# A two-block transformer kernel: modulation sums in the projection stage, an eighth early expert load, key products among transposes, and products moved from VectorE to ScalarE

## The chip, the cores and the metric

The kernel runs on one core of a Trainium2 chip. The metric is the time of one execution on the device in microseconds (us), the median of several runs. One execution is also taken by the hardware profiler, and all rows below come from that one. The engines are TensorE (PE; its weight loads are PEld), VectorE (DVE), ScalarE (ACT), GpSimd (POOL) and SyncE (SP, which here only issues DMAs). Data live in SBUF and in the matmul banks (PSUM).

## What is computed

Two blocks in a row on 512 latent tokens of width 1024, with 256 context tokens, in fp32. Cut to what the change touches:

```python
def first_block(x, c, ctx, c_ctx, w_mod, b_mod, ...):
    m_lat = split(silu(c) @ w_mod + b_mod, 6)        # six vectors of 1024 for the latent
    m_ctx = split(silu(c_ctx) @ w_mod + b_mod, 6)    # six for the context
    h_lat = modulate(rmsnorm(x), m_lat[0], m_lat[1]); h_ctx = ...
    mix   = token_mixers(h_lat @ w_in, h_ctx @ w_in) # neighbourhood and differential attention, gated deltanet, Fourier mix
    x = x + m_lat[2] * (mix @ w_out)
    h = modulate(rmsnorm(x), m_lat[3], m_lat[4])
    x = x + m_lat[5] * expert_choice_ffn(h, w_router, w_gate, w_up, w_down)   # 16 experts, 64 tokens each
    return rmsnorm(x)

def second_block(x, c, ctx, c_ctx, w_mod_2, ...):
    sh1, sc1, gt1, sh2, sc2, gt2 = split(silu(c) @ w_mod + b_mod, 6)          # shifts and scales of the context: only the first two
    h = rmsnorm(x) * (1 + sc1) + sh1;  p = h @ w_in
    y_ssd = ssd_bidir(p)         # chunked scan in both directions: scores = (C B^T) * exp(decay)
    y_att = softmax(q k^T, window, context keys, sink) v
    x = x + gt1 * merge(y_ssd, y_att)
    x = x + gt2 * conv_ffn(rmsnorm(x) * (1 + sc2) + sh2)
    return rmsnorm(x)
```

Vectors 3 and 4 of both modulations are wanted for the latent alone.

## The kernel before, in words

The program runs through stages, each a Python generator that writes instructions; `weave` (L321) takes the generators of a stage in turn, always the one with the smallest sum of the fractions that it has yielded so far. That order, and a scheduler that sorts by readiness within it, decide what stands behind what on each engine; every engine then runs its own queue strictly in order. The stages that matter, with their times in the profiled execution:

- **Projection**, about 120 to 221 us, the end of `g_proj` (L701). The input goes through `w_in` in blocks of 256 columns. Each block's weights (the DRAM tensor is `in_cola`, 512 KB a load into `base`) are split into a high and a low fp32r half on ScalarE (cast, L1963) and on VectorE or GpSimd (difference, L1964), and each product is three matmuls, hi·hi, hi·lo, lo·hi. SP issues the raw loads in program order.
- **Fourier mix and neighbourhood attention**, about 221 to 452 us, while the gated deltanet (`g_dn`, 40 rounds of short matmuls on `bank_dn`, a chain from round to round) and the modulation vectors (`g_mods`, L652) run beside it. `g_mods` makes ten vectors of 1024, each in two halves of 512 columns. `mod_rows` (L510) loads a half in four pieces of 512 KB into a ring named `mods` and multiplies the two conditioning columns with it, 8 fp32 matmuls of 32x512 (two records each in the trace) in four row groups; `mod_cols` (L521) turns the four groups with four transposes a half (L528) and adds them up on VectorE; `mod_cols_pk` (L533) does that with eight 64x128 matmuls by the identity into `bigbank`; `mod_bcast` (L545) spreads a vector over the partitions. Each step yields 0.1.
- **Differential attention**, 452 to 640 us, with 56 more rounds of the deltanet, then `w_out` and the router.
- **Experts** (`g_b`, L1617), 741 to 1692 us. Each of the 16 takes twelve loads of 2 MB (`in_w_gate`, `in_w_up`, `in_w_down`). A list `more` hands buffers of finished stages to the ring of loads; seven loads are issued before the first expert starts. `pair` (L1596) gathers the 2 x 64 tokens of two experts with an indirect DMA into a tile `Y` and turns them with 8 transposes. Up to 1297 us the context part of the second block's scan (`g_c0`) runs beside.
- **Tail of the experts** (`c_tile`, L2035), to 1740 us: each of the four token tiles is added to the residual, normed twice, and after the fourth `to_hT2` (L1974) turns all tiles, 32 transposes of 128x128, with scale and shift on ScalarE (L1987), a cast on VectorE (L1989) and a difference on VectorE or GpSimd (L1990). Then `c_att` begins with the keys: `tok2` (L2004), 48 matmuls of 128x256 for two token tiles.
- **Attention and scan of the second block** (`weave(self.c_att(Q), self.c_ssd(Q))`, L2719), 1740 to 2370 us. In `c_att` the softmax weights of two heads are divided by their sums on VectorE (L2171, 64 instructions of 128x512 or 128x640) ahead of their transposes (L2181). In `c_ssd` `weights(k)` (L2418) makes the decay weights of a channel pair and chunk, and `mixed(k)` (L2434) uses them:

```python
nc.scalar.activation(E[:, h], rw[:, h, 1], AF.Identity, bias=gc(1, 1, h))                        # L2424
nc.vector.scalar_tensor_tensor(E[:, h], rw[:, h, 0], gc(1, 0, h), E[:, h], ...)                  # L2426
nc.scalar.activation(E, E, AF.Exp)                                                              # L2427
nc.vector.tensor_scalar(W[:, h], cb[:, c, 0], gc(0, 0, h), None, op0=OP.mult)                    # L2429
nc.vector.scalar_tensor_tensor(W[:, h], cb[:, c, 1], gc(0, 1, h), W[:, h], op0=OP.mult, op1=OP.add)  # L2430
nc.gpsimd.tensor_mul(W, W, E)                                                                   # L2431
```

  `mixed` puts into `bank_y`, for each pair, chunk and head, `xs` times `W` and the chunk's state part `of` times the identity, two fp32 matmuls of 64x128 (two records each in the trace).
- **Output and FFN**, 2370 us to the end.

## Time and profile before

| | |
|---|---|
| median of 3 runs | 2982.91 us (2982.39 to 2989.98) |
| profiled execution: its time | 2982.76 us |
| profiled execution: its span | 2980.9 us |
| PE busy | 2770.4 us, 93% of the span |
| DVE, ACT, POOL busy | 1334.9 us (45%), 902.3 us (30%), 625.7 us (21%) |
| DMA | 658.53 MB, mean 221 GB/s |

Shares over the whole span mix stages with different limits, so the stages are read one by one. In the rows below, "busy" of a group is the time in which at least one of its instructions ran; matmuls are pipelined, so the mean of one is longer than what one adds. The bracket or the text behind the second bar says how long the engine was idle just before these instructions, and what released it. `L399` is the line of the helper that records nearly every matmul, so matmuls are told apart by their tiles.

### The profile page before, as it was taken

How to read it: one execution, taken by the hardware profiler on the slowest of the kernel's cores; microseconds unless marked ns; L12 is line 12 of the kernel's file. 1: busy time of each engine (PE TensorE's matmuls, PEld its weight loads, DVE VectorE, ACT ScalarE, POOL GpSimd, SP SyncE). 2: the span in 40 equal slices, each digit the busy share in tenths (PEclk: the TensorE clock that was granted, in tenths of full speed). 3: DMA queues.
4: the chain of work that ended last, by engine and by line, in shares of the span. 5: the costliest groups of instructions: out<-in, count | busy, mean ns of one | idle time of the engine just before them, and what ended most of it. 6: DMA issues, size and time to landing. Idle time of an engine off the chain costs nothing.

```text
span 2980.9 us, 41808 instructions
## 1 busy us (share of the span) xinstructions
PE 2770.4 (93%) x16824; PEld 1776.0 (60%) x16824; DVE 1334.9 (45%) x2654; ACT 902.3 (30%) x1836; POOL 625.7 (21%) x660
## 2 busy tenths in 40 slices
PE   7999989997999999988888789999999899999998
PEld 4894547765334333332222267777777688888886
DVE  5522445655121211111101167878787854454445
ACT  5511225532111010100000044545454543343333
POOL 3121224531000000000000024232323322332222
PEclk9999999998999999999999999999999999999999
DMA  6216661038999999989999923324242464242331
GB/s 268 75 34 200 209 218 32 30 121 309 397 430 430 429 429 430 429 371 430 431 431 430 387 88 105 118 64 123 72 120 74 134 232 160 94 154 95 97 99 57
DMA packets 213122, 658.53 MB, mean 221 GB/s; under 512 B 13816, under 2 KB 131192, under 8 KB 188352
## 3 DMA queue, kind: packets, MB, share of 16 engines
q1 hardware_dynamic: 185504, 601.73, 52.4%
q10 hardware_dynamic: 26272, 49.93, 4.7%
q0 software_dynamic: 1152, 4.19, 0.3%
q8 instruction: 133, 2.18, 0.3%
q14 instruction: 61, 0.50, 0.1%
HBM read 632.07 MB, written 23.73 MB: 220 GB/s over the span
## 4 chain that ended last, share of the span: by engine, by line
PE 68%; DMA 16%; DVE 10%; issue 2%; ACT 2%; POOL 2%; SPq 1%; ACTq 0%; POOLq 0%; DVEq 0%
PE bank_mm L399 29%; PE bigbank L399 20%; DMA l<-in_w_up 6%; PE bank_pj L399 6%; DMA l<-in_w_down 4%; PE bank_c L399 4%; PE bank_dn L399 2%; DMA mods<-in_cola 2%; DMA l<-in_w_gate 1%; PE bank_sm L399 1%; DVE base L2426 1%; DVE mix L2430 1%; PE bank_dnr L399 1%; DVE mix L2429 1%; PE bank_mm L2181 1%
## 5 line engine op out<-in xcount | busy, mean ns | idle before, releaser
L399 PE MATMUL bank_pj<-c,c 128*128 128x512 f32 (+2 forms) x1368 | 319.7, 376 | 0.3 <-DVE c L1964 0.3
L399 PE MATMUL bank_mm<-c,c 128*128 128x512 f32 (+1 forms) x1608 | 304.4, 347 | 4.9 <-ACT b L1987 3.2
L399 PEld LDWEIGHTS bank_mm<-c,c 128*128 128x128 f32 x1608 | 259.3, 191 | 44.2 <-ACT b L1987 3.6
L399 PE MATMUL bigbank<-l 128*64 128x512 f32 (+1 forms) x1104 | 266.1, 594 | 17.9 <-DMA l<-in_w_up 13.1
L399 PEld LDWEIGHTS bank_pj<-c,c 128*128 128x128 f32 (+1 forms) x1368 | 225.7, 189 | 50.7 <-issue 17.5
L1963 ACT CAST c<-base 128x1024 fp32r<-128x1024 f32 x147 | 152.8, 1045 | 254.3 <-PE bigbank L399 105.7
L1964 POOL TENSOR_TENSOR c<-base,c 128x1024 fp32r<-128x1024 f32 x47 | 116.7, 2483 | 472.9 <-ACT c L1963 404.6
L1964 DVE TENSOR_TENSOR c<-base,c 128x1024 fp32r<-128x1024 f32 x100 | 136.3, 1365 | 136.8 <-ACT c L1963 133.7
L399 PEld LDWEIGHTS bigbank<-l 128*64 128x64 f32 (+1 forms) x1104 | 80.9, 141 | 175.8 <-issue 140.4
L1692 DVE TENSOR_TENSOR b<-l,bigbank 128x512 f32<-128x512 f32 x32 | 20.5, 683 | 340.8 <-PE bigbank L399 293.5
L1691 ACT ACTIVATE l<-bigbank 128x512 f32<-128x512 f32 x32 | 17.4, 595 | 423.7 <-PE bigbank L399 423.7
L399 PE MATMUL bank_mm<-l 128*64 128x512 f32 (+2 forms) x528 | 124.8, 601 | 9.1 <-DMA l<-in_w_down 8.0
L399 PE MATMUL bigbank<-out,c 128*128 128x512 f32 x480 | 113.8, 397 | 1.9 <-ACT out L2524 1.8
L399 PE MATMUL bank_c<-b 128*128 128x256 f32 (+3 forms) x496 | 110.0, 373 | 1.9 <-ACT b L425 0.8
L399 PE MATMUL bank_mm<-h,sp 128*128 128x512 f32 (+3 forms) x544 | 105.5, 382 | 4.3 <-ACT h L644 3.8
L399 PEld LDWEIGHTS bank_dn<-dn 64*64 64x64 f32 x1920 | 74.8, 134 | 55.0 <-issue 39.3
L399 PEld LDWEIGHTS bigbank<-out,c 128*128 128x128 f32 x480 | 91.7, 192 | 23.0 <-ACT out L2524 2.2
L399 PE MATMUL bigbank<-b,l 128*64 128x512 f32 x352 | 84.9, 614 | 21.8 <-DMA b<-in_w_up 10.9
L1717 DVE TENSOR_TENSOR b<-bank_mm,ab 64x512 f32<-64x512 f32 x16 | 10.9, 683 | 208.1 <-PE bank_mm L399 208.1
L1786 ACT ACTIVATE b<-bank_c,base 128x256 f32<-128x256 f32 x20 | 11.3, 563 | 304.6 <-PE bank_c L399 304.6
L399 PEld LDWEIGHTS bank_c<-b 128*128 128x128 f32 (+1 forms) x496 | 80.4, 188 | 37.2 <-issue 23.9
L399 PE MATMUL bigbank<-c,ffn 128*128 128x512 f32 x432 | 100.3, 390 | 0.0
(538 smaller groups left out, 5060.7 us busy)
## 6 DMA issues: line engine op xcount, KB each, us to landing
l<-in_w_up SPq DMA_DIRECT2D x36, 2048.0 KB, 14.6
l<-in_w_down SPq DMA_DIRECT2D x31, 2048.0 KB, 17.0
l<-in_w_gate SPq DMA_DIRECT2D x29, 2048.0 KB, 18.2
mods<-in_cola SPq DMA_DIRECT2D x80, 512.0 KB, 4.9
base<-in_w_in SPq DMA_DIRECT2D x68, 512.0 KB, 3.7
b<-in_w_gate SPq DMA_DIRECT2D x15, 2048.0 KB, 34.0
base<-in_w_gate SPq DMA_DIRECT2D x13, 2048.0 KB, 16.9
wo<-in_w_up SPq DMA_DIRECT2D x13, 2048.0 KB, 33.8
```

The source lines that it names most:

```text
L399: self.mm_ins = self.nc.tensor.matmul(out, l, r, start=start, stop=stop).ins
L1691: nc.scalar.activation(s, ac[0][:, j], AF.Silu)
L1692: nc.vector.tensor_mul(hid[:, 512 * j:512 * j + 512], s, ac[1][:, j])
L1717: nc.vector.tensor_mul(Y[pp, 0:512], dn[0:64], gt2[0:64, 0:512])
L1786: nc.scalar.activation(y, b, AF.Identity, scale=wc(1), bias=self.col(bname, i))
L1963: nc.scalar.copy(hi, raw)
L1964: (nc.vector if self.wn % 4 in self.losplit else nc.gpsimd).tensor_sub(lo, raw, hi.bitcast(F32))
L2181: nc.tensor.transpose(tb[:, z], p[:, 128 * (g0 + z):128 * (g0 + z) + 128], self.ident)
L2426: nc.vector.scalar_tensor_tensor(E[:, h], rw[:, h, 0], gc(1, 0, h), E[:, h], op0=OP.subtract, op1=OP.min)
L2429: nc.vector.tensor_scalar(W[:, h], cb[:, c, 0], gc(0, 0, h), None, op0=OP.mult)
L2430: nc.vector.scalar_tensor_tensor(W[:, h], cb[:, c, 1], gc(0, 1, h), W[:, h], op0=OP.mult, op1=OP.add)
```

## The change

1. **Modulation sums.** Vectors 3 and 4 of both modulations leave `g_mods`. A new generator `g_late_mods` makes their eight halves in `g_proj`, which calls `next(sums)` at 16 places of the projection stage. A half loads eight pieces of 128x512 (256 KB each, on SP, a ring of four buffers); VectorE multiplies and accumulates five of them, ScalarE multiplies three, GpSimd adds these and the two partial sums (`mod_sums`); `mod_close` then sums over the partitions with 8 matmuls of 64x1 or 4 of 128x1 by a column of ones. Only the latent's conditioning column is used. A half is closed one half later. `g_mods` keeps six vectors, in the order 2, 5, then 0, 1, 2, 5 of the second modulation, with a yield of 1/6.
2. **Early load.** `more` gets `out_b` as an eighth buffer; the gather of a pair goes into `gt1_b`, one buffer, and the transposes read it there, so a pair's gather waits for the transposes of the pair before.
3. **Keys.** `c_tile` turns tiles 0 and 1 after the third tile; after the fourth it writes the transposes of tiles 2 and 3 between the 48 key matmuls of tiles 0 and 1 (in a bank `c0`), and ScalarE copies that bank to `self.rr`, which `c_att` then reads.
4. **ScalarE.** The first product of the decay weights (L2429, 128 instructions) and one of the two softmax divisions of each pair of heads (32 of 64) go from VectorE to ScalarE as copies with a scale.
5. **State part.** `mixed` puts `of` into `bank_y` with four 128x128 transposes for each pair, 64 in all, in place of 128 matmuls of 64x128 by the identity; `xs` times `W` accumulates on them.

```diff
-    def mod_cols_pk(self, s, wdram, bi, j, ring, rows, out):
-        nc = self.nc
-        t = self.big().rearrange("p (k g r) -> p k g r", k=8, g=4)
-        for h in range(2):
-            r = rows()
-            self.mod_rows(s, wdram, 2 * j + h, ring, r)
-            for kt in range(8):
-                self.mm(t[64 * h:64 * h + 64, kt].rearrange("p g r -> p (g r)"), r[:, kt::8], self.ident)
-        nc.vector.tensor_reduce(out, t[:, :, :, 0:2].rearrange("p c g r -> p c r g"), AX.X, OP.add)
-        nc.vector.tensor_add(out, out, self.col("b_mod_pk", 8 * bi, 8)[:, :, None].to_broadcast([128, 8, 2]))
...
+    def mod_sums(self, s, wdram, j, rings):
+        nc, (wr, da, pa, pp) = self.nc, rings
+        wv = self.block(wdram, j)
+        d, o = da(), pa()
+        for kt in range(8):
+            w, c = wr(), s[:, kt, 0:1]
+            self.ld(w, wv[:, kt])
+            if kt == 0:
+                nc.vector.tensor_scalar(d, w, c, None, op0=OP.mult)
+            elif kt in (1, 3, 6):
+                z = o if kt == 1 else pp()
+                nc.scalar.activation(z, w, AF.Copy, scale=c)
+                if kt > 1:
+                    nc.gpsimd.tensor_add(o, o, z)
+            else:
+                nc.vector.scalar_tensor_tensor(d, w, c, d, op0=OP.mult, op1=OP.add)
+            if kt == 3:
+                yield
+        nc.gpsimd.tensor_add(o, o, d)
+        self.msum = o
+    def mod_close(self, o, h, bias, out, pk):
+        p, n = (slice(64 * h, 64 * h + 64), slice(0, 8)) if pk else (slice(0, 128), slice(4 * h, 4 * h + 4))
+        t = self.bank((128, 8), "md")
+        for c in range(8 if pk else 4):
+            self.mm(t[p, n.start + c:n.start + c + 1], o[:, c::8] if pk else o[:, c * 128:(c + 1) * 128], self.km("one", 1))
+        self.nc.vector.tensor_add(out[p, n], t[p, n], bias[p, n])
+    def g_late_mods(self, P):
+        s1, s2 = self.s1b.ap(), self.s2b.ap()
+        mp, mc = self.mpk_b.ap(), self.m2c_b.ap()
+        of = [Ring(P, [512], 2, more=[Buf(self.M, [512]) for _ in range(2)])] + [Ring(self.M, [512], n) for n in (1, 2, 1)]
+        owed = []
+        for s, w, j, name, n, out, pk in ((s1, "w_mod", 3, "b_mod_pk", 0, mp[:, 0, :, 0], True), (s1, "w_mod", 4, "b_mod_pk", 8, mp[:, 1, :, 0], True),
+                                          (s2, "w_mod_2", 3, "b_mod_2", 24, mc[:, 2, :, 0], False), (s2, "w_mod_2", 4, "b_mod_2", 32, mc[:, 3, :, 0], False)):
+            for h in range(2):
+                yield from self.mod_sums(s, w, 2 * j + h, of)
+                if owed:
+                    owed.pop()()
+                owed.append(lambda o=self.msum, h=h, n=n, name=name, out=out, pk=pk: self.mod_close(o, h, self.col(name, n, 8), out, pk))
+                yield
+        owed.pop()()
+        for z in of:
+            for b in z.b:
+                b.free()
...
-            self.mod_bcast(s1, wm, I["b_mod"], 2, wr, rows, self.gt1_b.ap(), self.sel)
-            yield 0.1
-            self.mod_cols_pk(s1, wm, 0, 3, wr, rows, mp[:, 0])
-            yield 0.1
-            self.mod_cols_pk(s1, wm, 1, 4, wr, rows, mp[:, 1])
             nc.vector.scalar_tensor_tensor(a2, mp[:, 1, :, 0], 1.0, self.col("norm2_g_pk", 0, 8), op0=OP.add, op1=OP.mult)
-            yield 0.1
-            self.mod_bcast(s1, wm, I["b_mod"], 5, wr, rows, self.gt2_b.ap(), self.sel)
-            yield 0.1
+            for j, g in ((2, self.gt1_b), (5, self.gt2_b)):
+                self.mod_bcast(s1, wm, I["b_mod"], j, wr, rows, g.ap(), self.sel)
+                yield 1 / 6
...
-            for i, j in enumerate((0, 1, 3, 4)):
-                self.mod_cols(s2, wm, "b_mod_2", j, wr, rows, mc[:, i])
-                yield 0.1
+            for j in range(2):
+                self.mod_cols(s2, wm, "b_mod_2", j, wr, rows, mc[:, j])
+                yield 1 / 6
...
+                cr.free()
+                cr2.free()
+                sums = self.g_late_mods(P)
+            if t % 2 == 0:
+                next(sums)
...
-        cr.free()
-        cr2.free()
+        for _ in sums:
+            pass
...
-        nc.gpsimd.indirect_dma_start(Y, None, self.xnd, bass.IndirectOffsetOnAxis(self.ix[:, pr:pr + 1], 0))
+        nc.gpsimd.indirect_dma_start(G, None, self.xnd, bass.IndirectOffsetOnAxis(self.ix[:, pr:pr + 1], 0))
         yield
         for k4 in range(2):
             b = self.bank((128, 4, 128))
             for kk in range(4):
-                nc.tensor.transpose(b[:, kk], Y[:, 4 * k4 + kk::8], self.ident)
+                nc.tensor.transpose(b[:, kk], G[:, 4 * k4 + kk::8], self.ident)
...
-        more = [None, None, sum_b.ap(), None, None, None, in_b.ap()]
+        more = [None, None, sum_b.ap(), None, None, None, in_b.ap(), out_b.ap()]
...
+        mc, a = self.m2c_b.ap(), self.ab2_b.ap()
+        turned = lambda i: self.g_hT2([c["xn"][:, 2 * i], c["xn"][:, 2 * i + 1]], i, a[:, 0], mc[:, 0, :, 0], c["u"], lambda: self.bank((128, 2, 256)))
+        if t == 2:
+            for _ in turned(0):
+                pass
         if t == 3:
-            mc, a = self.m2c_b.ap(), self.ab2_b.ap()
+            last, kb = turned(1), self.bank((128, 2, 256), "c0")
             for i in range(2):
-                self.to_hT2([c["xn"][:, 2 * i], c["xn"][:, 2 * i + 1]], i, a[:, 0], mc[:, 0, :, 0], c["u"], lambda: self.bank((128, 2, 256)))
+                self.tok2(self.pre[0], i, 1, b=kb[:, i:i + 1])
+                for _ in range(3 if i == 0 else 1):
+                    next(last)
+            for _ in last:
+                pass
+            self.cp(self.rr.rearrange("p (t n) -> p t n", t=2), kb, "a")
...
-                b = self.tok2(w, t, 2)
+                b = self.rr.rearrange("p (t n) -> p t n", t=2) if half + t == 0 else self.tok2(w, t, 2)
...
-                for i in range(2):
-                    nc.vector.tensor_scalar(u["p"][i], u["p"][i], ri[:, i:i + 1], None, op0=OP.mult)
+                nc.vector.tensor_scalar(u["p"][0], u["p"][0], ri[:, 0:1], None, op0=OP.mult)
+                nc.scalar.activation(u["p"][1], u["p"][1], AF.Copy, scale=ri[:, 1:2])
...
-                    nc.vector.tensor_scalar(W[:, h], cb[:, c, 0], gc(0, 0, h), None, op0=OP.mult)
+                    nc.scalar.activation(W[:, h], cb[:, c, 0], AF.Copy, scale=gc(0, 0, h))
...
-                    ys[pr] = self.bank((128, 512), "y")
+                    b = ys[pr] = self.bank((128, 512), "y")
+                    for z in range(4):
+                        nc.tensor.matmul(b[:, 128 * z:128 * z + 128], of[:, z, 128 * pr:128 * pr + 128], self.ident, start=z == 0, stop=False, is_transpose=True)
                 yb, W, tk = ys[pr], Ws.pop(k), slice(128 * c, 128 * c + 128)
-                for z in range(2):
-                    for h in range(2):
-                        o = 128 * pr + 64 * h
-                        self.mm(yb[64 * h:64 * h + 64, tk], (of if z else xs)[:, c, o:o + 64], self.ident if z else W[:, h], z == 0, z == 1)
+                for h in range(2):
+                    o = 128 * pr + 64 * h
+                    self.mm(yb[64 * h:64 * h + 64, tk], xs[:, c, o:o + 64], W[:, h], False, c == 3)
```

TensorE in the projection, near its middle; `h_...` and `sp_...` are the split halves of the input and of a weight block, `bank_md` is the bank of the sums. Before:

```order
L399 MATMUL bank_mm<-h_117,sp_350 128x512
L399 MATMUL bank_mm<-h_116,sp_354 128x512
L399 MATMUL bank_mm<-l_105,a_109 128x24 x4
L399 MATMUL bank_mm<-h_118,sp_349 128x256
L399 MATMUL bank_mm<-h_119,sp_349 128x256
```

and now, with one of the eight closes among the matmuls of a block:

```order
L399 MATMUL bank_mm<-h_117,sp_350 128x512
L399 MATMUL bank_mm<-h_116,sp_354 128x512
L399 MATMUL bank_mm<-l_105,a_109 128x24 x4
L399 MATMUL bank_md<-base_59,l_105 64x1 x8
L399 MATMUL bank_mm<-h_118,sp_349 128x256
L399 MATMUL bank_mm<-h_119,sp_349 128x256
```

The other rows kept their places. TensorE at the end of the experts; `b_...` holds the token tiles, `c_...` the split weights of the keys and the split transposed tiles. Before:

```order
L1983 MATMUL bank_mm_9728<-base2_59,b1_6410 128x128
L1983 MATMUL bank_mm_9739<-base2_59,b1_6410 128x128
L1983 MATMUL bank_mm_9728<-base2_59,b1_6410 128x128 x3
L1983 MATMUL bank_mm_9739<-base2_59,b1_6410 128x128 x3
L1983 MATMUL bank_mm_9750<-base2_59,b1_6410 128x128 x4
L1983 MATMUL bank_mm_9761<-base2_59,b1_6410 128x128 x4
L399 MATMUL bank_mm_9830<-c4_9616,c1_9613 128x256
L399 MATMUL bank_mm_9830<-c8_9620,c1_9613 128x256
L399 MATMUL bank_mm_9830<-c4_9616,c2_9614 128x256
```

and now, in a piece of the keys, where the transposes of tiles 0 and 1 are already behind:

```order
L399 MATMUL bank_c0_9770<-c8_9662,c1_9655 128x256
L399 MATMUL bank_c0_9770<-c4_9658,c2_9656 128x256
L399 MATMUL bank_c0_9770<-c5_9659,c1_9655 128x256
L399 MATMUL bank_c0_9770<-c9_9663,c1_9655 128x256
L2036 MATMUL bank_mm_9806<-base2_59,b1_6452 128x128
L399 MATMUL bank_c0_9770<-c5_9659,c2_9656 128x256
```

The sixteen transposes of tiles 2 and 3 now stand among and behind the keys, one each behind 8, 14 and 21 of the 48, nine behind 38, four behind all. VectorE in the scan, between two heads' softmax; `mix_989x` to `mix_990x` before and `mix_993x` to `mix_994x` now are the decay tables and `W`, `bigbank` holds scores. Before, with L2429:

```order
L2448 TENSOR_TENSOR base_95<-bank_y,base_95 128x512
L2426 SCALAR_TENSOR_TENSOR base_95<-mix_9900,mix_9891,base_95 128x128 x2
L2429 TENSOR_SCALAR mix_9905<-mix_9898,mix_9891 128x128 x2
L2430 SCALAR_TENSOR_TENSOR mix_9905<-mix_9898,mix_9891,mix_9905 128x128 x2
L2159 TENSOR_REDUCE base_77<-bigbank 128x1
L427 COPY mix_9827<-bank_mm 128x512
L2160 TENSOR_SCALAR base_75<-base_77,mix_9811 128x1
L2426 SCALAR_TENSOR_TENSOR base_95<-mix_9901,mix_9891,base_95 128x128 x2
L2429 TENSOR_SCALAR mix_9902<-mix_9898,mix_9891 128x128 x2
L2430 SCALAR_TENSOR_TENSOR mix_9902<-mix_9898,mix_9891,mix_9902 128x128 x2
```

and now, where L2491 and L2495 are the lines L2426 and L2430 of before:

```order
L2514 TENSOR_TENSOR base_95<-bank_y,base_95 128x512
L2495 SCALAR_TENSOR_TENSOR mix_9946<-mix_9941,mix_9934,mix_9946 128x128 x2
L2491 SCALAR_TENSOR_TENSOR base_95<-mix_9942,mix_9934,base_95 128x128 x2
L2495 SCALAR_TENSOR_TENSOR mix_9947<-mix_9941,mix_9934,mix_9947 128x128 x2
L2224 TENSOR_REDUCE base_77<-bigbank 128x1
L427 COPY mix_9918<-bank_mm 128x512
L2491 SCALAR_TENSOR_TENSOR base_95<-mix_9943,mix_9934,base_95 128x128
L2225 TENSOR_SCALAR base_75<-base_77,mix_9903 128x1
L2491 SCALAR_TENSOR_TENSOR base_95<-mix_9943,mix_9934,base_95 128x128
L2495 SCALAR_TENSOR_TENSOR mix_9948<-mix_9941,mix_9934,mix_9948 128x128 x2
```

The rows of L2429 are gone from VectorE's queue; they stand in ScalarE's as L2494.

## Rows read from the trace of the kernel before

**Rows 1.** Stretches: length, busy us per engine (records), granted clock, DMA share.

```profile
120.00:221.50 101.50, 101.50 (x830) 94.81 (x829) 25.22 (x79) 20.97 (x37) 21.20 (x25) 1.00 0.12 39
...
221.50:452.00 230.50, 212.84 (x2083) 112.77 (x2082) 92.48 (x222) 56.34 (x173) 50.01 (x84) 1.00 0.64 206
...
452.00:640.00 188.00, 180.51 (x2290) 137.57 (x2290) 120.07 (x299) 105.05 (x289) 92.36 (x151) 0.98 0.10 33
...
741.00:1297.00 556.00, 538.38 (x2302) 215.08 (x2302) 99.65 (x193) 62.25 (x128) 28.65 (x28) 0.99 0.98 415
...
1740.00:2370.00 630.00, 598.93 (x4016) 478.12 (x4016) 506.05 (x1157) 301.90 (x701) 188.04 (x210) 0.99 0.32 95
```

**Rows 2.** TensorE's groups, 221-452 us: count | busy us, mean ns | idle before.

```profile
L399 PE MATMUL bank_mm<-mods,ab 128*32 128x512 f32 x320 | 71.5, 603 | 11.7 <-DMA mods<-in_cola 11.2 <-DVE dn L427 0.3 <-ACT dn L425 0.2
...
L399 PE MATMUL bigbank<-base,mods 128*64 128x128 f32 x64 | 8.7, 288 | 0.0
...
L528 PE MATMUL bank_mm<-base,mods 128*128 128x128 f32 x32 | 5.2, 285 | 0.0
```

**Rows 3.** TensorE's waits, 221-452 us: total us, times, longest.

```profile
PE bank_mm L399 <- DMA mods<-in_cola: 11.2, 15, 2.1
```

**Rows 4.** Groups of TensorE, ScalarE and GpSimd, 110 to 222 us.

```profile
L399 PE MATMUL bank_mm<-base,l 128*64 128x4 f32 x96 | 3.0, 199 | 0.0
...
L399 PE MATMUL bank_mm<-l,a 128*128 128x24 f32 x8 | 1.0, 258 | 0.0
...
L730 ACT ACTIVATE l<-l 128x512 f32<-128x512 f32 x2 | 1.3, 629 | 0.0
...
L1964 POOL TENSOR_TENSOR sp<-base,sp 128x1024 fp32r<-128x1024 f32 x6 | 14.3, 2392 | 61.9 <-ACT sp L1963 61.9
```

**Rows 5.** DMA issues, 120-222 us: count, KB each, median us to landing.

```profile
base<-in_cola SPq DMA_DIRECT2D x6, 512.0 KB, 3.7
```

**Rows 6.** SyncE's queue, 125-222 us: start, length, what, count.

```profile
131.56 34.47 SPq L430 DMA_DIRECT2D base<-in_cola  x6
```

**Rows 7.** Waits of TensorE, 742 to 1289 us.

```profile
PE bigbank L399 <- DMA l<-in_w_up: 1.3, 1, 1.3
...
PE bigbank L399 <- DMA l<-in_w_gate: 1.0, 1, 1.0
...
PE bank_mm L399 <- DMA l<-in_w_down: 0.6, 1, 0.6
```

**Rows 8.** Time line, 1720-1760 us: start, length, what [idle before, releaser].

```profile
1738.94 1.02 ACT L1987 ACTIVATE b<-bank_mm,base,base 128x256 f32<-128x256 f32 x2 [0.38 <-POOL c L1990]
...
1740.01 7.51 PE L399 MATMUL bank_mm<-c,c 128*128 128x256 f32 x48 [3.19 <-ACT b L1987]
```

**Rows 9.** Four stretches of the last attention part, summed.

```profile
sum 337.00, PE 310.44 PEld 231.81 DVE 316.27 ACT 170.98 POOL 126.28; mean PE 77.61 PEld 57.95 DVE 79.07 ACT 42.75 POOL 31.57
```

**Rows 10.** The same four stretches: line 2429, line 2171 and tile bank_y alone, summed.

```profile
sum 337.00, DVE 39.64; mean DVE 9.91
...
sum 337.00, DVE 27.28; mean DVE 6.82
...
sum 337.00, PE 39.16 PEld 30.27 DVE 10.20; mean PE 9.79 PEld 7.57 DVE 2.55
```

**Rows 11.** Groups of TensorE, VectorE and ScalarE, 1745 to 2370 us.

```profile
L2181 PE MATMUL bank_mm<-base,mix 128*128 128x128 f32 x280 | 43.4, 282 | 3.7 <-DVE mix L2171 3.0 <-ACT mix L425 0.4 <-DVE mix L427 0.2
...
L2399 DVE SCALAR_TENSOR_TENSOR mix<-base,mix 128x512 f32<-128x512 f32 x32 | 22.0, 689 | 0.0
...
L2424 ACT ACTIVATE base<-mix,mix 128x128 f32<-128x128 f32 x128 | 46.6, 395 | 52.8 <-POOL mix L2431 50.7 <-DMA mix<-csum 1.2 <-ACT base L2424 0.4
...
L2162 ACT ACTIVATE mix<-bigbank,base 128x512 f32<-128x512 f32 x32 | 22.0, 687 | 38.3 <-DVE base L2160 31.6 <-PE bank_sm L399 3.4 <-DVE base L2426 1.6
```

**Rows 12.** Groups of GpSimd, 1978 to 2065 us.

```profile
L2386 POOL TENSOR_TENSOR mix<-mix,mix 128x512 f32<-128x512 f32 x4 | 5.1, 1276 | 6.5 <-PE bank_sm L399 6.5
...
L1964 POOL TENSOR_TENSOR c<-base,c 128x1024 fp32r<-128x1024 f32 x1 | 3.4, 3352 | 0.0
```

26 lines of the change are left out of this document (21 added, 5 removed).

## The prediction

> **What bounds the kernel now.** I read the stretches of the program first, then in each stretch that the change touches the groups of instructions and what ended TensorE's waits. In the projection TensorE is busy 101.5 of 101.5 us while VectorE, ScalarE and GpSimd have 21 to 25 us of work each and the DMA share is 0.12 [rows 1]: matmuls set the time, and everything else has room. From 221.5 to 452 us TensorE is busy 212.8 of 230.5 us; of the 17.7 idle, 11.2 are waits for pieces of modulation weights [rows 1, 3]. So there, too, matmuls set the time, and the modulation is part of them. Among the experts to 1297 us TensorE has 538.4 of 556 us and the DMA engines 0.98 [rows 1]: both are nearly full. From 1740 to 2370 us TensorE has 598.9 of 630 us [rows 1], but that is an average of two kinds of stretches. In 1828-1905, 1978-2065, 2127-2210 and 2278-2368 us, 337 us together, VectorE is busy 316.3 (94%) and TensorE 310.4 (92%) [rows 9]; the rest has TensorE at 598.9 - 310.4 = 288.5 of 293 us. VectorE sets the pace in the four stretches, TensorE in the others.
>
> **Modulation, what goes.** Four of ten vectors leave the stretch from 221.5. Of the 320 matmul records 128 go, 71.5 x 128/320 = 28.6 us; all 64 records on `bigbank`, 8.7; half of the transposes, 2.6 [rows 2]. That is 39.9 us of TensorE. The waits for weights belong to the same loads, so four tenths of 11.2 [rows 3], 4.5, can go too: 44 at most. What is late next is the deltanet: its 40 rounds have 230.5/40 = 5.8 us each now and would have 4.7, with less to put beside them. The differential stage runs 56 rounds in 188 us, 3.4 each, with TensorE busy 180.5 [rows 1], so a round can be shorter than 4.7. I take 40; were the remaining 13 us of idle time to double, 31 would be left.
>
> **Modulation, what comes.** The projection gets 48 close matmuls of one column, 96 records. 64 have 64-wide weights, as the 128x4 group has (3.0/96 = 0.031 us): 2.0. 32 have 128-wide weights, as the 128x24 group has (1.0/8 = 0.125): 4.0 [rows 4]. All 6 us lie on the path. The rest is meant to lie beside: a half takes VectorE 5 x 0.69 = 3.4 us [rows 11], ScalarE 3 x 0.63 = 1.9 [rows 4], GpSimd 3 x 1.28 = 3.8 [rows 12], against some 90 us from 131.6, where SP issues the last six weight loads [rows 6], to 221.5, or 11.2 us a half. The loads go through four buffers in two rounds. A piece of 256 KB has no row; one of 512 KB lands in 3.7 us [rows 5], so two rounds with a VectorE pass each take at most 2 x (3.7 + 0.7) = 8.8 us, under 11.2, and a half is closed one half later. Behind the new instructions stand, on SP, the six raw loads, and on ScalarE, VectorE and GpSimd the splits of the next weight block (GpSimd's 2.39 each [rows 4]); with three engines about a quarter busy I count 1 us of stalls for the first closes, which have the least time. So -7. Ends: -3 (all 96 records at 0.031), -14 (each of eight closes stalls 1 us more).
>
> The Trainium skill, DMA: Bandwidth & Descriptors, section on the anatomy of one DMA, gives about 2.0 us fixed plus bytes over 436 GB/s for a DMA; a 256 KB piece would land in an estimated 2.6 us, two rounds would take 6.6, and by this page the stall of 1 us would be nil and the sum 1 us lower. No row shows a load of that size.
>
> **The early load.** A load that starts earlier helps where TensorE would wait for one. Between 742 and 1289 us it does so three times, 1.3 + 1.0 + 0.6 = 2.9 us [rows 7]; one load of 2 MB at 415 GB/s [rows 1] is 5 us. I take 2.5, with ends -1 (the second pair's gather, which now waits for the first pair's transposes) and 5 (if the stretch behind 1297 also gains the whole load).
>
> **Keys.** The 48 matmuls of 7.5 us start at 1740.0, behind 3.2 us of waiting for ScalarE's scales [rows 8]. Now they stand among the transposes, so at most 7.5 us go. But the first half's scales (0.51 each [rows 8]) stand ahead of the fourth tile's own norms in ScalarE's queue; six of them are 3 us by which that tile's transposes, and the end, come later. I take 7.5 - 3 = 4.5, ends 0 and 7.
>
> **Scan and attention.** In the four stretches VectorE loses L2429, 39.6 us, and half of L2171, 13.6 [rows 10]: 316.3 - 53.2 = 263. TensorE loses the state part of `bank_y`, half of 39.2 [rows 10], and gets 64 transposes of 43.4/280 = 0.155 us [rows 11], 9.9: 310.4 - 9.7 = 301. ScalarE gets 128 products of the shape of L2424, 46.6 us in all, and of the divisions in these stretches some 22 of 0.69 as L2162 [rows 11], 15: 171 + 62 = 233. So TensorE becomes the bound there, and at most 337 - 301 = 36 us can go. Outside TensorE reaches 98.5% beside a busy VectorE; at that share the stretches take 305 (gain 32), at 95.5% 315 (22). Since every `W` now goes through ScalarE once more before VectorE can go on, I take 20. The low end is that the 27 us of TensorE's idle time stay and some 4 are added: 6. Outside the four stretches TensorE is the bound already and I count nothing.
>
> **Sum.** 40 - 7 + 2.5 + 4.5 + 20 = 60. The profiled execution took 2982.76 us, 1.9 of them outside its span of 2980.9, and stands within 0.2 of the median 2982.91. 2982.8 - 60 = 2923.
>
> **Rivals.** *A, the deltanet's chain takes the place of the modulation's matmuls.* For: TensorE has idle time there already, and filler goes from beside 40 rounds in a chain. Against: 3.4 us a round in the next stage. If a round can't go under 5.5 us, 40 rounds take 220 us, the 40 become 10, and the time is 2953.
>
> *B, ScalarE's order takes VectorE's place.* For: the queue is strict, and exponentials and casts that others wait for now stand behind the copies; of L2424's idle time 50.7 us is already spent waiting for L2431 at the end of the same chain [rows 11], which becomes one step longer. Against: ScalarE would be at 233 of some 315 us, 74%. If the idle time of TensorE grows by the 9.7 us that its work shrinks, the 20 become 0: 2943.
>
> *C, slower: the closes wait for their sums.* A close sits in TensorE's strict queue ahead of the next matmuls. If SP reaches a half's loads only when TensorE is almost at its close, because they stand behind a raw load that waits for its buffer (SP's six loads are spread over 34 us [rows 6]), a half lays bare its two rounds and the GpSimd adds, 8.8 + 3.8 = 12.6 us, eight times 101. Without the projection's cost the change gives 67, so this decides from 67/8 = 8.4 us a half, and at the full price the time is 2983 - 67 + 101 = 3017. Against: DMA share 0.12, and a half's delay of every close.
>
> On GpSimd the rows show 2.39 us for L1964 in the projection and 3.35 for the one in 1978-2065, where VectorE is nearly always busy [rows 4, 12], 1.4 times as long. The Trainium skill, GPSIMD Engine Reference, section Specifications, says that GpSimd shares its SBUF interfaces with VectorE and contends with VectorE instructions that have two SBUF inputs, which the four accumulations of a half have; the rows agree in direction. By that rule the adds of C take 1.4 x 3.8 = 5.3 and the time of C is 3029; where they are hidden it changes nothing.
>
> *The change doesn't do what it says in part:* if the eighth buffer comes free only after the seventh load has landed, the 2.5 go and the time is 2925, which the range holds.
>
> **How the numbers follow.** Forecast 0.66, A 0.13, B 0.14, A and B together 0.03 (gain 10, 2973), C 0.03, something else without gain 0.01. A measurement of this kernel can tell about 0.3%, 9 us, from no change. Faster: 0.66 + 0.13 + 0.14 = 0.93; slower 0.03; the same 0.04, with A and B together at that bound. All good ends at once give 44 - 3 + 5 + 7 + 32 = 85, 2898; all bad ones 31 - 14 - 1 + 0 + 6 = 22, 2961. Neither comes all at once; A at 2953 and B at 2943 lie inside with a few us around them, so the range is 2898 to 2958.
>
> **What would show it.** The stretch of Fourier mix and neighbourhood attention should last about 190 us and not 220 (A), with under 8 us of waits for modulation weights. The projection should last about 108 us with TensorE nearly full; waits of `bank_md` for GpSimd's sum of several us each would be C. The waits for expert weights before 1289 us should nearly vanish, and the scan should start some 5 us earlier after the experts' end. The stretches in which VectorE was at 94% should add up to some 317 us with TensorE above 94%, VectorE near 83% and ScalarE near 74%; TensorE below 92% with waits for ScalarE or for L2431's successor is B. I am wrong if the stages before 452 us together gain less than 20, or if the last attention part gains less than 6.

## The result, and the profile after

The changed kernel takes 2946.07 us (median of 4 runs, 2939.43 to 2948.90) against 2985.20 (4 runs, 2982.39 to 2989.98): the ratio is 0.9864, 95% interval 0.9841 to 0.9887, or 34 to 47 us less. The forecast was 60 less. The profiled execution of after took 2939.43 us, 43 less than that of before, and is the fastest of the four: its mean granted TensorE clock was 0.987, that of the other three 0.982 to 0.983, so the tables below show the change at its best. Page of after, engines:

```profile
PE 2738.9 (93%) x16520; PEld 1760.3 (60%) x16520; DVE 1326.5 (45%) x2527; ACT 975.8 (33%) x2018; POOL 660.2 (22%) x684
```

The table compares the two profiled executions between the same instructions, found in TensorE's time lines. Each row ends at the instruction named.

| stage, up to | before | after | difference | forecast |
|---|---|---|---|---|
| projection: from 120 us to the first `bank_dn<-a,l` | 99.1 | 116.7 | +17.6 | +7 |
| Fourier mix, neighbourhood attention: the last `mods` matmul | 233.6 | 182.1 | -51.5 | -40 |
| differential attention: its last scores | 187.2 | 194.0 | +6.8 | 0 |
| router: the first expert matmul | 103.3 | 102.3 | -1.0 | 0 |
| experts and their tail: the first `bank_pj` | 1004.2 | 997.0 | -7.2 | -7 |
| attention and scan: the first `bigbank<-out,c` | 628.5 | 621.9 | -6.6 | -20 |
| output and FFN: the last `bigbank<-c,ffn` | 595.6 | 593.9 | -1.7 | 0 |

The same stretches of after, in the columns of [rows 1]:

```profile
120.00:236.72 116.72, 115.19 (x863) 107.01 (x861) 66.47 (x127) 35.94 (x58) 56.41 (x47) 0.97 0.52 173
236.72:418.78 182.06, 178.02 (x1837) 97.38 (x1837) 84.53 (x202) 51.55 (x164) 48.67 (x83) 1.00 0.52 167
418.78:612.82 194.04, 184.98 (x2393) 141.59 (x2392) 122.41 (x304) 107.47 (x296) 93.66 (x153) 0.98 0.11 34
...
1712.06:2333.93 621.87, 590.95 (x3801) 464.40 (x3801) 464.64 (x1002) 365.75 (x869) 188.70 (x211) 0.99 0.33 98
```

TensorE is still nearly always busy in the projection, but VectorE went from 25.2 to 66.5 us and the DMA share from 0.12 to 0.52. In the attention and scan VectorE is at 75%, ScalarE at 59%, and TensorE still stands idle 30.9 us. TensorE's groups in the projection of after:

```profile
L399 PE MATMUL bank_md<-base,l 128*64 128x1 f32 x64 | 8.3, 259 | 0.0
...
L399 PE MATMUL bank_md<-base,l 128*128 128x1 f32 x32 | 3.8, 240 | 0.0
L399 PE MATMUL bank_mm<-base,l 128*64 128x4 f32 x96 | 3.4, 208 | 0.0
```

The closes (the rows of `bank_md`) are 8.3 + 3.8 = 12.1 us where the forecast had 6. In the next stage, groups and waits of TensorE, answering [rows 2, 3]:

```profile
L399 PE MATMUL bank_mm<-mods,ab 128*32 128x512 f32 x192 | 46.6, 604 | 2.4 <-DMA mods<-in_cola 2.3
L399 PE MATMUL bank_dn<-dn 64*64 64x64 f32 x798 | 37.5, 224 | 0.7 <-DVE dn L1063 0.6 <-ACT dn L425 0.2
```

```profile
PE bank_mm L399 <- DMA mods<-in_cola: 2.3, 5, 0.7
```

The waits for modulation weights fell from 11.2 to 2.3 us.

### The profile page after: what moved, and what is told of

It reads as the page before. It is cut to its first block, busy times and chain, and to the rows that moved or that the text cites. A ratio compares the mean times of both kernels' runs of the same rounds, so it can differ in the third digit from the quotient of the medians.

```text
span 2937.6 us, 41399 instructions
## 1 busy us (share of the span) xinstructions
PE 2738.9 (93%) x16520; PEld 1760.3 (60%) x16520; DVE 1326.5 (45%) x2527; ACT 975.8 (33%) x2018; POOL 660.2 (22%) x684
## 4 chain that ended last, share of the span: by engine, by line
PE 68%; DMA 15%; DVE 8%; issue 3%; ACT 3%; POOL 2%; SPq 0%; POOLq 0%; ACTq 0%; DVEq 0%
PE bank_mm L399 27%; PE bigbank L399 21%; PE bank_pj L399 6%; PE bank_c L399 4%; DMA b<-in_w_gate 4%; PE bank_dn L399 3%; DMA b<-in_w_down 2%; DMA l<-in_w_down 2%; PE bank_sm L399 1%; DMA l<-in_w_up 1%; DMA wo<-in_w_gate 1%; DMA l<-in_w_gate 1%; DMA mods<-in_cola 1%; PE bank_dn L1042 1%; DVE c L2013 1%
## 5 line engine op out<-in xcount | busy, mean ns | idle before, releaser
L399 PE MATMUL bank_mm<-c,c 128*128 128x512 f32 (+1 forms) x1560 | 296.8, 348 | 2.2 <-DVE c L2013 1.3
L399 PEld LDWEIGHTS bank_mm<-c,c 128*128 128x128 f32 x1560 | 251.9, 189 | 41.4 <-DVE c L2013 1.7
L399 PE MATMUL bigbank<-l 128*64 128x512 f32 (+1 forms) x1088 | 260.9, 589 | 14.7 <-DMA l<-in_w_up 11.2
L399 PEld LDWEIGHTS bigbank<-l 128*64 128x64 f32 (+1 forms) x1088 | 79.9, 140 | 169.7 <-issue 142.7
L399 PEld LDWEIGHTS bank_mm<-h,sp 128*128 128x128 f32 (+1 forms) x544 | 85.8, 186 | 24.7 <-ACT h L681 4.0
## 6 DMA issues: line engine op xcount, KB each, us to landing
wo<-in_w_gate SPq DMA_DIRECT2D x15, 2048.0 KB, 21.7
```

Source lines behind the costliest of these rows:

```text
L399: self.mm_ins = self.nc.tensor.matmul(out, l, r, start=start, stop=stop).ins
```

## Experiments

Kernels that do one part alone start from the kernel before, the others say from which. "Stage" times are between the same instructions as in the table above. Each ratio comes with its 95% interval in brackets. How far the granted clock differs between the runs stands at the end of this section; it bears on every difference of about 10 us or less.

**The sums alone.** All of the change's hunks in `g_mods`, `mod_sums`, `mod_close`, `g_late_mods` and `g_proj`, nothing else.

> The kernel before with the modulation sums alone (the first part of the change). Theory 1, the forecast's: the closes cost 6 us and 1 us of stalls in the projection, the next stage gives 40, the differential stage nothing: about -33 us, 2950. Theory 2, from the trace after: the closes cost 12 us of TensorE (0.13 us a record whatever the width), waits and a stretch at the lower clock 5 more, the next stage gives 51 of which 7 come back in the differential stage as deltanet rounds that moved there: about -27 us, 2956. The first deltanet matmul behind the projection starts some 17 us later than before under theory 2, 7 under theory 1.

Measured 2956.36 us (4 runs) against 2984.33, ratio 0.9902 (0.9880 to 0.9924): -28. The first deltanet matmul comes 19.4 us late, the last `mods` matmul 30.6 early, the last differential scores 24.0 early: theory 2, with the same three pieces (+, -, +) as in after.

**The keys alone.** The hunks in `to_hT2`, `tok2`, `c_tile` and the first line of the key loop of `c_att`.

> The kernel before with the keys between the transposes alone. Forecast -4.5 us (2979), ends 0 and -7. From the trace after, where the tail of the experts is 6.4 us shorter: -6.4 (2977). Rival: the tail of the experts is shorter for the earlier load or something before it, and alone it gives nothing (2983).

Measured 2983.38 us (10 runs) against 2984.33, ratio 0.9998 (0.9983 to 1.0014). In its trace the experts with their tail take 999.2 us, where the five kernels without this edit that were profiled by then and later (sums, both ScalarE kernels, state part, four buffers for E) take 1004.3 to 1006.8: the 6 us are there. But the stage behind is 632.1 against 628.5, and TensorE waits at its start:

```profile
PE bank_pj L399 <- ACT b L1991: 2.7, 1, 2.7
```

The first projections stand right behind the keys now, and wait for the last transposed half to be scaled; in after this wait is 1.2 us. A gain of up to 5 us by itself is neither shown nor excluded by the times.

**Both moves to ScalarE alone.**

```diff
-                for i in range(2):
-                    nc.vector.tensor_scalar(u["p"][i], u["p"][i], ri[:, i:i + 1], None, op0=OP.mult)
+                nc.vector.tensor_scalar(u["p"][0], u["p"][0], ri[:, 0:1], None, op0=OP.mult)
+                nc.scalar.activation(u["p"][1], u["p"][1], AF.Copy, scale=ri[:, 1:2])
...
-                    nc.vector.tensor_scalar(W[:, h], cb[:, c, 0], gc(0, 0, h), None, op0=OP.mult)
+                    nc.scalar.activation(W[:, h], cb[:, c, 0], AF.Copy, scale=gc(0, 0, h))
```

> The kernel before with both moves to ScalarE alone (first products and half of the divisions), the state part left as it was. Theory 1, VectorE was the bound of the four stretches: VectorE loses 53 of 316 us there, TensorE's 310 of 337 becomes the bound, at 96% 323: about -14 us (2969). Theory 2, TensorE waits there for the end of chains that pass through every engine, and the waits only change their last link: -2 to -5 us (2979).

Measured 2974.02 us (8 runs), ratio 0.9966 (0.9954 to 0.9978): -10, between the theories. The stage takes 618.1 us, with TensorE idle 22.6 instead of 33.5.

**The first products alone.** Only the second half of that diff.

> The kernel before with the first products of the decay weights on ScalarE alone, the divisions left on VectorE. They are 39.6 of the 53 us that VectorE loses in the four stretches, the divisions 13.6. If VectorE's busy time decides, three quarters of the gain of both: about -8 us (2976). If the waits decide, TensorE's 5.4 us of waits for divided softmax weights stay: -3 to -5 (2980), and the divisions carry the rest.

Measured 2982.48 us (10 runs) against 2984.06, ratio 0.9994 (0.9983 to 1.0005): at most 5 us, likely 2. VectorE loses 21.7 us of busy time in the stage (505.8 to 484.1), where both moves take 40.7 from it (to 465.1), and the stage is 3.4 us shorter. About half of VectorE's relief thus gave a sixth of the gain by the medians; half of the gain, 5 us, is the end of the interval, and a part of the difference is the granted clock (end of this section). Whether VectorE's busy time decides is not shown. What the divisions add is open too; they weren't run by themselves. They stand right ahead of transposes for which TensorE waited 5.4 us before, but that wait went with the products alone:

```profile
PE bank_mm L2181 <- DVE mix L2171: 5.4, 7, 2.4
```

```profile
PE bank_mm L2181 <- DVE mix L2171: 0.9, 2, 0.7
```

(before, and here). The waits were expected to stay if they were what held the stage; they fell, and nearly nothing came of it.

**The state part alone.** The last hunk, in `mixed`.

> The kernel before with the state part as transposes alone. Theory 1, VectorE is the bound in the four stretches, so 6 to 10 us less of TensorE give nothing there: 0 to -1 us (2982). Theory 2, TensorE's own work and the latency of chains set the time together: -3 to -6 us (2978).

Measured 2984.78 us (10 runs) against 2984.33, ratio 1.0006 (0.9992 to 1.0020): no gain shown, at most 2 us.

**The change without the state part.** The same hunk undone in after.

> The changed kernel with the state part back as 128 matmuls by the identity. Theory 1: TensorE is the bound in the scan and gets 6 to 10 us of work more: +6 to +10, 2952 to 2956. Theory 2: TensorE waits for chains there, and the four transposes at a pair's start only make it wait sooner: 0, 2946, within 3.

Measured 2944.50 us (4 runs), ratio to before 0.9873 (0.9850 to 0.9895), after's being 0.9864. The four transposes take work from TensorE, 594.6 to 591.0 us busy in the stage, and cost it waits, 24.3 to 30.9 idle. The rows of after name them, those for the tile that the four transposes begin among the largest:

```profile
PE bank_y L399 <- POOL mix L2496: 5.3, 10, 2.1
PE bank_sm L399 <- DVE base L2463: 5.0, 6, 1.4
PE bigbank L399 <- ACT mix L2227: 3.9, 5, 1.8
PE bank_mm L399 <- ACT mix L425: 3.6, 2, 2.4
...
PE bank_y L2504 <- DVE base L2514: 1.4, 1, 1.4
```

Without the state part the first of these is 2.1 us, and in place of the last stands a wait of 0.5.

**Four buffers for E, in after.**

```diff
+        e4 = Buf(P, [2, 2, 128]).ap()
         def E_r():
             E_i[0] += 1
-            return e2[:, E_i[0] % 2]
+            return (e2 if E_i[0] % 4 < 2 else e4)[:, E_i[0] % 2]
```

> The changed kernel with four instead of two buffers for the exponent tile E of the decay weights. After the change ScalarE still stands still 16.1 us because the buffer that its first step of a later weight writes (L2489) is still read by GpSimd's product (L2496), and everything behind it in ScalarE's queue waits too. Theory 2 (chains through ScalarE and GpSimd set the time in the scan): -3 to -10 us against the changed kernel, 2936 to 2943. Theory 1 (TensorE's own work, with some 5% it can't use): nothing, 2946.

Measured 2939.50 us (4 runs), ratio to before 0.9849 (0.9827 to 0.9870). The interval overlaps that of after, so a gain over after is not shown by the times; the stage is 616.3 us against 621.9, and TensorE's waits for GpSimd's product went from 5.3 to 3.2.

**Four buffers for E, in before.** The same edit.

> The kernel before with four instead of two buffers for E, nothing else. ScalarE there stands still 50.7 us for GpSimd's product of an earlier weight. If that chain, and not VectorE's busy time, held the four stretches: -4 to -12 us (2972 to 2980). If VectorE at 94% was the bound: 0 (2984).

Measured 2990.09 us (10 runs) against 2984.06, ratio 1.0019 (1.0008 to 1.0029): 6 us slower. ScalarE's waits for L2431 fell, as the edit intends,

```profile
ACT base L2424 <- POOL mix L2431: 50.7, 34, 4.9
```

```profile
ACT base L2426 <- POOL mix L2433: 17.8, 8, 4.5
...
ACT mix L2426 <- POOL mix L2433: 15.8, 13, 3.1
```

(the same line in the two kernels; the second row is for the two new buffers): from 50.7 us to 33.6, a third less, and no gain came of it. With the products on VectorE, that ring was not what held the stage. The 6 us go with a lower granted clock, 0.982 in the mean of these runs against 0.984; whether the edit lowers it is not shown.

**No closes.** From after; the kernel leaves the close matmuls out, and `mod_close` keeps one addition, so the four vectors hold a part of their sums.

```diff
-        t = self.bank((128, 8), "md")
-        for c in range(8 if pk else 4):
-            self.mm(t[p, n.start + c:n.start + c + 1], o[:, c::8] if pk else o[:, c * 128:(c + 1) * 128], self.km("one", 1))
-        self.nc.vector.tensor_add(out[p, n], t[p, n], bias[p, n])
+        m = 8 if pk else 4
+        self.nc.vector.tensor_add(out[p, n], o[p, :m], bias[p, n])
```

> The changed kernel with the close matmuls of the modulation sums left out: the four vectors get a part of a sum and their bias instead, so the output is another; all loads, products and sums stay. By the trace after, the 96 close records cost 12.1 us of TensorE and their sums about 1.5 us of waits elsewhere: -12 us, 2934. By the forecast's prices: -6, 2940. If the projection's extra time were the stretch at the lower clock and the waits, at most -2: 2944. Whether the stretch at the lower clock behind the 128x4 matmuls is still there tells whether the closes have to do with it.

Measured 2944.33 us (4 runs), ratio to before 0.9862 (0.9833 to 0.9891): no gain over after shown. The projection takes 118.7 us, as long as with the closes. TensorE's waits in it:

```profile
PE bank_mm L399 <- DVE l L427: 5.5, 4, 1.8
PE bank_mm L399 <- DVE l L874: 5.0, 3, 2.8
PE bank_mm L399 <- ACT l L544: 3.4, 1, 3.4
```

13.9 us of waits stand where 12.1 us of matmuls stood. VectorE's copies and rotations of projected blocks stand in its queue behind the sums, and the sums wait themselves:

```profile
DVE l L541 <- POOL l L551: 14.4, 6, 3.5
...
DVE l L548 <- DMA l<-in_cola: 5.3, 6, 1.8
DVE l L548 <- DMA sp<-in_cola: 5.3, 5, 3.7
DVE l L541 <- DMA l<-in_cola: 3.1, 1, 3.1
```

**No closes, and buffers that change places.** VectorE's first product of a half (L541) writes a partial sum that GpSimd reads last in the half before (L551).

```diff
-        d, o = da(), pa()
+        dz, o = [da(), pp()], pa()
+        self.swap = not getattr(self, "swap", False)
+        d, zb = dz if self.swap else dz[::-1]
...
-                z = o if kt == 1 else pp()
+                z = o if kt == 1 else zb
```

> The kernel without the close matmuls (their part of the output left out as there), and with VectorE's partial sum and ScalarE's product changing buffers from half to half, so that VectorE's first product of a half no longer waits until GpSimd has read the last partial sum (14 us of VectorE's waits there). Theory 1, the projection has two limits, TensorE's close matmuls and VectorE's strict queue, in which the copies that TensorE waits for stand behind the sums: the projection loses 5 to 12 us against the kernel without closes, 2932 to 2939. Theory 2, the landing of the 256 KB pieces is the second limit: nothing, 2944.

Measured 2939.16 us (4 runs), ratio to before 0.9846 (0.9826 to 0.9867). The projection is 112.2 us against 118.7, the wait of VectorE's first product for GpSimd 4.3 against 14.4, at the same granted clock of 0.97 in the projection. By the medians that is 5 us less than without the swap, at the low end of theory 1, though the two intervals overlap: the traces show two limits, one behind the other.

**Joined halves.** From after; a first-block vector is summed in one buffer of 1024 and closed at once with `o[:, c::8]` over 128 columns.

```diff
-        p, n = (slice(64 * h, 64 * h + 64), slice(0, 8)) if pk else (slice(0, 128), slice(4 * h, 4 * h + 4))
+        p, n = (slice(0, 128), slice(0, 8)) if pk else (slice(0, 128), slice(4 * h, 4 * h + 4))
...
                 owed.append(...)
                 yield
+                if pk:
+                    owed.pop()()
```

> The changed kernel in which the two halves of a first-block vector lie side by side and are closed together, 8 matmuls of 128x1 in place of 16 of 64x1, 64 of 96 records left; the close then comes half a vector's work sooner behind its sums. If a record costs 0.13 us whatever its width: -4 us, 2942. If the 64-wide ones cost 0.03 as the forecast had it: +1 to 0, 2946. If the closes now wait for their sums: slower than the changed kernel, by up to 5.

Measured 2957.82 us (4 runs), ratio to before 0.9915 (0.9894 to 0.9935): 12 slower than after. Groups and waits:

```profile
L399 PE MATMUL bank_md<-base,l 128*128 128x1 f32 x64 | 11.7, 309 | 8.8 <-POOL l L551 8.8
```

```profile
PE bank_md L399 <- POOL l L551: 8.8, 2, 5.4
```

The 64 records cost 11.7 us, about as much as 96 did. With 3.8 for the 32 that are as in after, the 32 joined ones take 7.9, an estimate of 0.25 us each and twice the 0.13 of the narrow ones: the width of a strided weight load counts. The clock is a rival, since both joined batches ran at a granted clock of 0.50 almost throughout:

```profile
154.40:158.40 4.00, 3.97 (x16) 0.50 0.36 131
182.00:186.00 4.00, 3.96 (x16) 0.55 0.21 66
```

But in the kernel without the state part the clock fell to 0.50 during the last half microsecond of a narrow batch, and its sixteen records took the same 2.08 us as those of the other three, so these loads are not the slower for it. The early closes wait 8.8 us for GpSimd's last addition. How much of the 12 us is the waits is not shown: the projection of this profile ran 20 us at a granted clock of 0.50, that of after 7, and the runs' mean clock was 0.980 against 0.984.

**All that helped.** After without the state part, with four buffers for E and with the sums' buffers changing places.

> The changed kernel with the state part as before, four buffers for E and the buffers of the sums changing places. Theory 2 for the scan, chains through ScalarE and GpSimd: the scan 12 to 16 us shorter than in the kernel before where the change has 7; 0 to 3 us from the sums; together 2932 to 2940. Theory 1, TensorE's own work in the scan: 2946 or above.

Measured 2936.92 us (5 runs, 2932.22 to 2938.17), ratio 0.9841 (0.9824 to 0.9857): 47 us less than before, 9 less than the change by the medians. The two intervals overlap, but each of these five runs is faster than each of after's four. The scan takes 611.7 us, TensorE idle 22.9, at a granted clock of 1.00.

The early load wasn't run alone; its effect is too small for the times, and the traces with it and the keys (996.3 to 998.8) stand beside 999.2 with the keys alone.

**The granted clock, a rival to every small difference.** The mean granted clock differs from run to run, and the time goes with it: over 51 runs of the kernel before, each microsecond of span times (1 - granted clock) came with 0.85 us of time. Span times granted clock is therefore an estimate of the time without the lower level, good to some 2 us; here as a difference to the same of before (2934, at a mean of 0.984).

| kernel | mean granted clock | span times clock |
|---|---|---|
| sums alone | 0.983 | -31 |
| keys alone | 0.985 | +4 |
| both moves to ScalarE alone | 0.985 | -6 |
| first products alone | 0.983 | -4 |
| state part alone | 0.983 | -2 |
| four buffers for E, in before | 0.982 | +1 |
| after | 0.984 | -39 |
| after without the state part | 0.984 | -41 |
| after with four buffers for E | 0.985 | -42 |
| no closes | 0.986 | -35 |
| no closes, swapped | 0.985 | -41 |
| joined halves | 0.980 | -39 |
| all that helped | 0.986 | -42 |

By this estimate the change and the sums keep their gains, the products come close to both moves, the keys alone cost, and joined halves and four buffers for E in before are not slower; of the 9 us of the last kernel about 3 remain, and of the 5 us of the swap about 6. It does not say whether an edit changes the clock, which would make the loss its own.

## Why the prediction was right, point by point

The time lies in the range and the sign is right; the forecast of 60 us was half as much again as the 39 that the medians show. Three of its terms were wrong: the closes in size, the early load, which gave nothing that shows, and the scan in its mechanism; and the range was wide: it holds every gain from 25 to 85. Part of the closeness is luck, since the step with the matmuls that go gave 5 us more than forecast and the projection and the scan 24 less.

**Modulation, what goes: right.** The matmuls of these groups fell by 36.2 us of the 39.9 counted (71.5 to 46.6, 8.7 to nothing, 5.2 to 2.6), the waits by 8.9 where 4.5 were counted. The stage fell by 51.5 us, more than counted, since some deltanet rounds moved on: its 64x64 records fell from 880 to 798 (22 a round, so nearly four rounds), those of the differential stage rose from 978 to 1060, and it got 6.8 us longer. Net -44.7, a little beyond the 44 that was called the most. The deltanet's chain did not take the matmuls' place; rival A fell.

**Modulation, what comes: 17.6 us for 7; the closes were wrong by 6.** The step that failed is "64 have 64-wide weights, as the 128x4 group has (3.0/96 = 0.031 us): 2.0". They took 8.3, 0.13 each. A better neighbour stood in [rows 2]: 64 records of `bigbank<-base,mods`, 8.7 us, also 64 wide and also read with every eighth column. The weight loads differ:

```profile
L399 PEld LDWEIGHTS bank_md<-base,l 128*64 128x64 f32 x64 | 8.0, 216 | 0.7 <-issue 0.4
L399 PEld LDWEIGHTS bank_md<-base,l 128*128 128x128 f32 x32 | 4.1, 191 | 0.2
L399 PEld LDWEIGHTS bank_mm<-base,l 128*64 128x64 f32 x96 | 3.3, 153 | 0.1
```

A contiguous 64-wide load takes 0.03 us of the path, a strided one 0.125, for two reasons. The records of the 128x4 group start in pairs, 7 ns within a pair and 58 ns from pair to pair, so two run side by side; those of the closes follow each other 120 ns apart. The rest is the stride: in the joined kernel, with 128 columns each, 32 contiguous records took 3.8 us and 32 strided ones 7.9.

Of the other 5 us, 1.5 are waits and 3.4 a stretch at the lower of the two clock levels: between 133 and 140 us the granted clock is 0.50 (1.2 GHz for 2.4). Whether that is the change's is open. Before lost nothing there; five more profiles with its projection lost 1.7 to 3.4 us, the eight with the sums 3.4 to 10.2.

Right behind the closes lay a second limit that the forecast had priced too low: VectorE's 5 x 0.69 = 3.4 us a half are 5.0 in the trace,

```profile
L548 DVE SCALAR_TENSOR_TENSOR l<-l,ab 128x512 f32<-128x512 f32 x16 | 16.1, 1003 | 9.7 <-DMA l<-in_cola 9.7
L548 DVE SCALAR_TENSOR_TENSOR l<-sp,ab,l 128x512 f32<-128x512 f32 x16 | 15.5, 971 | 1.0 <-DMA sp<-in_cola 0.7
L541 DVE TENSOR_SCALAR l<-l,ab 128x512 f32<-128x512 f32 x8 | 8.3, 1039 | 17.3 <-POOL l L551 14.2 <-DMA l<-in_cola 3.1
```

```profile
l<-in_cola SPq DMA_DIRECT2D x32, 256.0 KB, 3.4
sp<-in_cola SPq DMA_DIRECT2D x30, 256.0 KB, 3.8
base<-in_cola SPq DMA_DIRECT2D x6, 512.0 KB, 6.3
```

and a 256 KB piece lands in 3.4 to 3.8 us, about what [rows 5] shows for 512 KB with idle DMA engines. It is not the 2.6 us that the prediction worked out from the Trainium skill, DMA: Bandwidth & Descriptors, section on the anatomy of one DMA, which describes DMAs issued by GpSimd while these go out from SP; the rows decide. The slower accumulations, 1.00 and 0.97 us for the 0.69 of [rows 11], agree in direction with the rule of the Trainium skill, GPSIMD Engine Reference, section Specifications, on VectorE instructions with two SBUF inputs. No run here took GpSimd away, and L541, which reads one tensor, was slowed more, 1.04 us for the 0.49 of the same form at L2171 in before; that GpSimd is the cause is not shown. Rival C had the right place, the sums behind the closes, but its price never came: TensorE did not wait 8 us a half, it waited 1.5 in all, for VectorE's copies (L427, L876) and not for a sum.

**Early load and keys: right in the sum**, 7.2 against 7, but not in its parts. A load is on its way under the gather: right behind the first expert matmul the DMA engines move 221 GB/s (714 to 716 us) where before they stood still (742 to 748). But TensorE's waits for expert weights up to 1260 us are 1.2 and 0.9, 2.1 where [rows 7] has 2.9, and did not nearly vanish. From the first expert matmul to the last on `bigbank` the seven profiles without the early load take 980.8 to 984.2 us (before 982.0), the seven with it 981.8 to 983.6 (after 982.7), and the keys alone, which turn tiles 0 and 1 early as after does but load nothing early, take 982.9: the 2.5 forecast for the load did not come. The gain lies behind that, in the tail with the keys, 22.2 us before and 14.3 after, where 4.5 was forecast; of these 7.9 us 3.4 are less time lost to a lower clock (10.2 us at 0.50 before, 3.4 after). Alone, the keys gave 5 to 6 there, and the stage behind them took most of that back.

**Scan and attention: wrong, 6.6 for 20.** Other profiles bear the size out: the kernels with the scan of before took 625.4 (sums), 628.5 and 632.1 us (keys), those with the scan of after 620.9 to 621.9 (after, no closes, swapped, joined). So the gain is 3.5 to 11, and "if the last attention part gains less than 6" is not clearly passed.

Two steps failed. The first is "VectorE loses L2429, 39.6 us, and half of L2171, 13.6", 53.2 in all. Its busy time in the whole stage fell by 41.1 (505.8 to 464.6): the rows of one line count time in which other VectorE instructions run too. Of the 39.6 us, L2429 runs alone in 28.1, and taking it away freed 21.7.

The second is "So TensorE becomes the bound there": four stretches at 94% VectorE were taken as one. In the two that were cut further, each has two parts. Before and after, the state part and the weights part of these groups:

```profile
1830.00:1860.00 30.00, 26.92 (x112) 16.04 (x110) 29.50 (x64) 11.72 (x30) 13.52 (x18) 1.00 0.29 84
1860.00:1905.00 45.00, 40.50 (x355) 34.15 (x353) 42.08 (x112) 26.05 (x69) 18.71 (x17) 0.96 0.42 125
1980.00:2010.00 30.00, 28.16 (x133) 18.32 (x132) 29.13 (x68) 11.91 (x31) 14.27 (x17) 1.00 0.23 67
2010.00:2055.00 45.00, 41.66 (x344) 33.38 (x342) 42.13 (x113) 26.26 (x70) 16.81 (x16) 0.96 0.40 118
```

```profile
1795.00:1825.00 30.00, 27.18 (x111) 16.47 (x110) 28.07 (x52) 11.70 (x28) 14.51 (x18) 1.00 0.37 106
1825.00:1870.00 45.00, 40.95 (x306) 31.54 (x304) 32.48 (x85) 33.39 (x94) 14.95 (x17) 1.00 0.32 98
1945.00:1975.00 30.00, 26.23 (x123) 17.37 (x122) 28.70 (x54) 12.83 (x33) 13.65 (x15) 1.00 0.31 92
1975.00:2020.00 45.00, 43.74 (x334) 34.08 (x333) 35.41 (x90) 35.06 (x97) 16.82 (x17) 1.00 0.31 93
```

In the state parts (the 30-us rows) VectorE still has 28.1 and 28.7 of 30 us: of the 19.9 us of L2429 in these rows of before, 6.2 lay there and 13.7 in the weights parts. In the weights parts VectorE fell from 42 of 45 to 32 and 35, but TensorE rose only from 40.5 and 41.7 to 41.0 and 43.7; each row of before holds a stretch at the lower clock (0.96), without which it would be about 1.7 less. Over the 150 us VectorE came to the 83% that the prediction named as a sign, but TensorE stayed at 92% where it named 94, and ScalarE at 62% where it named 74. TensorE's waits in the whole stage were, before,

```profile
PE bigbank L399 <- ACT mix L2162: 7.1, 5, 2.3
PE bank_mm L2181 <- DVE mix L2171: 5.4, 7, 2.4
PE bank_mm L399 <- DVE mix L427: 5.2, 5, 2.0
```

and moved to GpSimd's product, ScalarE's copies and the state's steps (the rows of after under the change without the state part). Which of these links holds the stage is not shown.

Rival B's result (2943) came close to the time, but its mechanism did not come: TensorE's idle time, which was to grow by 9.7 us, went from 33.5 to 30.9. Of the later link that it named, the waits for GpSimd's product are there; four buffers for E gain 7 us behind the move by the medians, with overlapping intervals, and nothing before it. And the 9.7 us that TensorE was to lose by the state part were 3.6 in its busy time, against 6.6 of new waits.

## What to carry to other kernels

A stretch in which an engine is 94% busy must be cut until each piece has one kind of work before its relief is priced; what is moved counts only in the pieces it stood in, and only with the time in which nothing else ran on that engine. A neighbouring row is a price only if width and stride of the operands agree, and whether two instructions ran side by side. Before a few microseconds are put down to an edit, compare the granted clock of the runs. Where work goes beside an engine that is always busy, the queues that empty that engine's banks carry it too: here their order was a second bound, which showed only when the first was taken away.

## What the runs showed of the hardware

- A weight load of 64 fp32 columns that stand eight elements apart takes 0.125 us of the path, one of 128 neighbouring columns 0.13, one of 128 strided columns an estimated 0.25. One of 64 neighbouring columns took 0.03 where two ran side by side.
- The strided loads did not take longer at the lower clock: sixteen records took 2.08 us at a granted clock of 1.00, and the same where it was 0.50 for the last half microsecond (after without the state part, 140.6 to 142.7 us).
- VectorE overlaps neighbouring instructions: the 128 first products cover 39.6 us of the four stretches, but in only 28.1 of them does nothing else run on VectorE.
- TensorE's granted clock falls to 0.50 (1.2 GHz for 2.4) for 3.4 to 17.1 us at a time, several times in every profiled execution, at places that differ from kernel to kernel; half of such a stretch is lost where TensorE sets the time. Summed over the attention and scan the profiles lost from 0 us (the last kernel) to 10 (four buffers for E, in before); before and after lost 7.2 and 6.4 there. What TensorE did before a fall differs: 82 matmuls of four columns in 2.6 us (after, 133 us), a batch of closes of one column (after without the state part, at 142, 159, 173 and 187 us, one at each of the four strided batches), idle for 2.3 us (before, 2030 us). Other batches of closes were followed by none, and what decides stays open.
